# A fifth seven-product pair in the second column half of Down, and a new order of its pairs

## The chip, the cores and the metric

The kernel runs on one core of a Trainium2 chip. Its time is the device time in microseconds (us), the median of several runs. TensorE (PE in the profile) does the matmuls, PEld are its weight loads, VectorE is DVE, ScalarE is ACT, GpSimd is POOL, and SyncE (SP) issues the loads.

## The reference, cut to what matters

One block of a streaming encoder on x of 256 frames by 2048 features, in float32: a half-step SwiGLU FFN, a mixing part (gated DeltaNet and chunked attention, merged), and a second half-step FFN. The FFN is what matters here:

```python
def swiglu(h, w_gate, w_up, w_down):
    return (jax.nn.silu(h @ w_gate) * (h @ w_up)) @ w_down

h = rms_norm(x, ffn1_norm[l])
x = x + 0.5 * swiglu(h, ffn1_w_gate[l], ffn1_w_up[l], ffn1_w_down[l])
```

with a hidden width of 5504. The last matmul, by w_down, is called Down.

## The kernel before

**Products of float32 numbers.** Each weight and each activation is split into a high part and a low part in a rounded format, `hi` (a cast by ScalarE) and `lo = src - hi` (a subtraction by VectorE). A product (`product`, L456) is three matmuls, hi x hi (L462), hi x lo (L463), lo x hi (L464), each with a 128x128 activation block as the loaded operand and 512 columns of weights as the moving one.

**Pairs, plain and fast.** The contraction runs over k tiles of 128, two at a time: a pair. With the two blocks of 128 frames and two groups of 512 columns, a pair is a 2x2 by 2x2 product of blocks. A plain pair does it in eight block products (24 matmuls of 512 columns). A fast pair does it in seven (21 matmuls), by sums and differences of blocks in the manner of Strassen and Winograd. A fast pair needs sums of the activation blocks (`act_sums`, and for Down `bank_sums`, L573) and of the weight blocks.

**Preparing the weights of a pair.** `load` (L344) takes a buffer `raw` and has SP fetch the pair's weights, 1 MB in two DMAs. `begin` (L362) does the rest up to ScalarE's casts, and `prepare` (L426) the subtractions:
- plain: one cast `wh` (L380) and one subtraction `wl` (L434), each 128x2048; three buffers (raw, wh, wl);
- fast: three VectorE operations for the sums `s` (L406 to L408), casts of two pieces of raw (`w`, `v`, L411) and of `s` (`sh`, L413), and the subtractions `w`, `v` and `sl` (L434); five large buffers (raw, s, w1, sh, sl) and a small one of a ring of two (v).

**The order.** `plan` (L279) lists all pairs in order of use with a flag plain or fast, and a step takes the next one. Weights are loaded up to two pairs ahead of the one being prepared. Which buffer and which place in an engine's queue an operation gets is settled when the program is built. All large tiles come from one ring of 22 buffers, 8 KB per partition each (`heap`, L61): the weights, the activations x of the FFN (four fast pairs with a buffer each, four plain ones with half a buffer each), four hidden tiles of a chunk, and the block sums of hidden pairs (two pairs to a buffer).

**The FFN (L593).** Groups of 512 hidden columns run through gate/up (`gate_up`, eleven groups in all), in chunks of 4, 4 and 3 groups (`CHUNKS`). Behind each chunk comes its part of Down. The first two chunks have 16 k tiles, that is, pairs 0 to 7; their Down does the 2048 output columns in two halves, d = 0 and d = 2, of two groups of 512 columns each. Each half is one call of `seven` (L489): it takes the pairs in the order `js`, those in `fast` by seven products. Behind the last fast pair the banks that only fast pairs use are combined on ScalarE and VectorE (L531 to L535) while the remaining plain pair runs; the results leave by accumulating DMAs of GpSimd (L628). Behind the second half the next chunk's gate/up groups follow; the first two of a chunk have four fast pairs each (0, 2, 4, 6), the others three (0, 2, 4).

Before, both halves of a 16-k-tile chunk had the fast pairs 2, 3, 5, 6. The first half took the pairs in the order 0, 1, 2, 4, 3, 7, 5, 6 and the second in their natural order. The hidden tiles' transposes and block sums are jobs (`hidden`, L597) that run some steps behind gate/up, the last two of a chunk in the first steps of Down's first half.

In the profile Down's outputs are `pd`, gate/up's `pf`, hidden tiles `hid`, their block sums `hs`, the sums' scratch `shid`, the FFN's x `xf` (fast) and `xr` (plain).

Of the kernel before, what the change touches and what calls it, by code (L numbers as in the profile page):

```python
# [20 lines left out]
KD = D // P  # L21
# [9 lines left out]
FOUR = (0, 2, 4, 6)  # L31
DOWN = (2, 4, 6)
SECOND = (1, 3, 0, 2, 4, 5, 6, 7)
DEEP = (2, 3, 5, 6)
LAST = (1, 3)
APART = (0, 1, 2, 4, 3, 7, 5, 6)
FIRST = (1, 3, 5, 7, 0, 2, 4, 6)
QUAD = {2: (0, 0), 3: (1, 0), 4: (0, 1), 8: (1, 1)}
CHUNKS = ((0, 4), (4, 8), (8, 11))
# [5 lines left out]
def block_kernel(ctx: ExitStack, tc: tile.TileContext, a: dict, out: bass.AP):  # L45
# [220 lines left out]
    FG = [(c, min(4, KF - c)) for c in range(0, KF, 4)]  # L266
# [6 lines left out]
    def pairs_of(f, i):  # L273
        return range(KD // 2) if i else FIRST if f == "1" else SECOND

    def down_pairs(a0, a1):
        return DEEP if a1 < len(FG) else LAST

    def plan():  # L279

        for f in "12":
            for a0, a1 in CHUNKS:
                for i in range(a0, a1):
                    c, m = FG[i]
                    js = pairs_of(f, i)
                    gu = zip(*(t_pieces(a[w + f], c, m, 0, KD, [2 * j for j in js]) for w in ("wg", "wu")))
                    for j, p in zip(js, gu):
                        yield j in fast_pairs(f, i), p
                k0, k1 = FG[a0][0], sum(FG[a1 - 1])
                cols = lambda d, js=None: t_pieces(a["wd" + f], 4 * d, 4, k0, k1, js and [k0 + 2 * j for j in js])  # L290
                for d in (0, 2):
                    if a1 < len(FG):
                        js = range(KD // 2) if d else APART
                        yield from sevens(cols(d, js), cols(d + 1, js), DEEP, js)
                    elif d == 0:
                        yield from sevens(cols(0), cols(1), LAST, range(6))
                    else:
                        yield from twos(cols(2))
                        yield from twos(cols(3))
            if f == "2":  # L300
                return
            yield from mixing()
# [5 lines left out]
    def sevens(one, two, fast=DOWN, pairs=range(KD // 2)):  # L308
        for j, pieces in zip(pairs, zip(one, two)):
            yield j in fast, pieces  # L310
# [178 lines left out]
    def seven(nm, n, fast, act, jobs=(), feed=None, pairs=range(KD // 2), out=None, base=None, kt=KD):  # L489

        size = {b: len(fast) for b in range(1, 9)}
        for b in (2, 3, 4, 8):
            size[b] += kt - 2 * len(fast)
        size[8] -= len(fast)
        done = dict.fromkeys(size, 0)
        banks = {}

        def add(b, act, wt):  # L500
            if b not in banks:
                banks[b] = (acc_bank if b < 5 else core_bank)(f"p{nm}_{b}")[:, :n]
            done[b] += 1
            product(banks[b], act, wt, done[b] == 1, done[b] == size[b])

        ev = {}
        idle = 0
        for at_pair, j in enumerate(pairs):
            if j in fast:
                ps = take_weights()  # L510
                for at, (b, i7, w) in enumerate(ps):
                    add(b, act(j, i7), w)
                    if at == 3:
                        tick()
            else:
                for s in range(2):
                    wh, wl, _ = take_weights()
                    if feed and s == 0:
                        feed(at_pair)
                    for k, w in enumerate(zip(wh, wl)):  # L520
                        for t in range(2):
                            add((2, 4, 3, 8)[2 * s + t], act(j, 2 * k + t), w)
                    idle += 1
                    if idle > 3 and jobs and j > max(fast, default=-1):
                        jobs.popleft()()
                    while at_pair == KD // 2 - 1 and s == 1 and jobs:
                        jobs.popleft()()
            if fast and j == fast[-1]:
                idle = 1
                g0, u0, g1, u1 = (wide(f"e{nm}_{x}", n) for x in range(4))  # L530
                nc.scalar.copy(g0, banks[1])  # L531
                nc.vector.tensor_add(u0, banks[6], g0)
                nc.vector.tensor_add(g1, banks[7], u0)
                nc.vector.tensor_add(u1, banks[5], g1)
                nc.vector.tensor_add(u0, banks[5], u0)  # L535
                ev = {2: g0, 3: u0, 4: g1, 8: u1}
                if base:
                    for b, x in base.items():
                        nc.vector.tensor_add(ev[b], x, ev[b])
        if out:  # L540
            for b, put in out.items():
                put(ev[b])
                e = wide(f"e{nm}_{b}", n)
                nc.scalar.copy(e, banks[b])  # L544
                put(e)
            return None
        if not fast:
            return banks
        for b in (2, 3, 4, 8):
            nc.vector.tensor_add(ev[b], banks[b], ev[b])  # L550
        return ev
# [41 lines left out]
    def ffn(nm, xr, nxt, feed):  # L593
        f = "1" if nxt else "2"
        jobs = deque()

        def hidden(hb, us, m, c0, more):  # L597

            for c, mm, ps in turn(lambda t: us[t][:, c0 * P :], min(2, m - c0), f"{hb.name}_{c0}"):
                dst = hb[:, c0 : c0 + mm]  # L600
                split_to(dst[:, :, 0, :], dst[:, :, 1, :], ps)
                if more is not None:
                    bank_sums(ps, more, f"{hb.name}_{c0}")

        for a0, a1 in CHUNKS:
            hid, fast, sums, half = [], down_pairs(a0, a1), {}, None
            for i in range(a0, a1):
                m = FG[i][1]
                us = gate_up(nm, f, i, xr, jobs, feed if i == 0 else None)
                hb = heap([P, 4, 2, T], F32R, f"hid{nm}_{i}")  # L610
                hid.append(hb)
                for c0 in range(0, m, 2):
                    j = 2 * (i - a0) + c0 // 2
                    if j in fast:
                        half = heap([P, 2, 2, 4, P], F32R, f"hs{nm}_{i}{j}") if half is None else half
                        sums[j], half = (half[:, 0], half) if len(sums) % 2 == 0 else (half[:, 1], None)
                    jobs.append(lambda hb=hb, us=us, m=m, c0=c0, s=sums.get(j): hidden(hb, us, m, c0, s))
            n = 3
            while jobs:
                after(n, jobs.popleft())  # L620
                n += 1
            last = a1 == len(FG)
            act = quads(hid)
            block = lambda j, b: act(2 * j + b // 2, b % 2) if b < 4 else [sums[j][:, s, b - 4] for s in range(2)]
            kt = sum(FG[a1 - 1]) - FG[a0][0]
            for d in (0,) if last else (0, 2):
                out = {
                    b: lambda e, dst=xd[d + dd][t]: nc.gpsimd.dma_start(dst, e, accum_op=ALU.add)  # L628
                    for b, (dd, t) in QUAD.items()
                }  # L630
                js = range(6) if last else range(KD // 2) if d else APART
                seven(f"d{nm}_{a0}{d}", 512, fast, block, pairs=js, out=out, kt=kt)
            if not last:
                continue

            def again(d):
                xs = fetch(d, f"{nm}{a0}")
                if nxt:
                    nxt.square(d, xs)
                    after(3, lambda: nxt.turn(d, xs))  # L640
                else:
                    after(3, lambda: store(d, xs))

            for d in range(2):
                after(3 + d, lambda d=d: again(d))
            for d in range(2, 4):
                pd = pair(f"pd{nm}_{a0}{d}")
                xs = fetch(d, f"{nm}{a0}")
                gemm(pd, sum(FG[a1 - 1]) - FG[a0][0], act, 512)
                for t in range(2):  # L650
                    nc.vector.tensor_add(xs[t], xs[t], pd[t])
                if not last:
                    put(xs, d)
                elif nxt:
                    norm(nxt, d, xs)
                elif d < 3:
                    after(3, lambda d=d, xs=xs: store(d, xs))
                else:
                    store(d, xs)
# [620 lines left out]
    block = lambda j, b: mq(2 * j + b // 2, b % 2) if b < 4 else [ms[j][:, s, b - 4] for s in range(2)]  # L1280
# [91 lines left out]
```

## Time and profile before

| what | value |
| --- | --- |
| time, median of 3 runs | 2103.79 us (2103.19 to 2105.52) |
| the profiled execution: span from first to last instruction | 2101.9 us |
| granted TensorE clock | 1.000 |
| PE busy, matmuls | 2086.3 us (99%), 9711 |
| PEld busy | 1738.0 us (83%) |
| DVE busy | 1837.8 us (87%), 2074 instructions |
| ACT busy | 1205.7 us (57%) |
| POOL busy | 78.8 us (4%) |
| HBM | 407.72 MB read, 28.32 MB written |

No time is listed for the profiled execution beside its span; the span stands 1.9 us under the median of the runs. A row of the timeline gives the start, the duration, the engine, the line, the operation, the tiles as out<-in, the shapes, and a count; in brackets stands the idle time of the engine ahead of it and who ended it. In a table by stretches the columns are the length of the stretch and each engine's busy time with its count of instructions. A row of the view by groups gives busy time, mean duration in ns, and idle time ahead of it. Rows of waits give the total, the count and the longest.

### The profile page before, as it was taken

How to read it: one execution, taken by the hardware profiler on the slowest of the kernel's cores; microseconds unless marked ns; L12 is line 12 of the kernel's file. 1: busy time of each engine (PE TensorE's matmuls, PEld its weight loads, DVE VectorE, ACT ScalarE, POOL GpSimd, SP SyncE). 2: the span in 40 equal slices, each digit the busy share in tenths (PEclk: the TensorE clock that was granted, in tenths of full speed). 3: DMA queues.
4: the chain of work that ended last, by engine and by line, in shares of the span. 5: the costliest groups of instructions: out<-in, count | busy, mean ns of one | idle time of the engine just before them, and what ended most of it. 6: DMA issues, size and time to landing. Idle time of an engine off the chain costs nothing.

```text
span 2101.9 us, 25811 instructions
## 1 busy us (share of the span) xinstructions
PE 2086.3 (99%) x9711; PEld 1738.0 (83%) x9711; DVE 1837.8 (87%) x2074; ACT 1205.7 (57%) x1254; POOL 78.8 (4%) x93
## 2 busy tenths in 40 slices
PE   8999999999999999999999999999999999999999
PEld 6888788887898988888888888888887888888897
DVE  6998999989997788877885787999989999889994
ACT  6755565646555655657555555556555555556552
POOL 0000110002001000000010000000000200011001
PEclk9999999999999999999999999999999999999999
DMA  9655895649858755644554466767655975569576
GB/s 317 219 189 181 246 270 196 206 148 277 254 189 247 256 183 178 225 156 142 164 179 159 143 201 219 236 200 226 213 188 169 283 236 194 180 189 309 178 224 161
DMA packets 399932, 437.73 MB, mean 208 GB/s; under 512 B 14896, under 2 KB 372544, under 8 KB 399552
## 3 DMA queue, kind: packets, MB, share of 16 engines
q1 hardware_dynamic: 388288, 415.12, 61.2%
q0 software_dynamic: 11520, 20.98, 5.8%
q8 instruction: 76, 1.25, 0.3%
q14 instruction: 48, 0.39, 0.1%
HBM read 407.72 MB, written 28.32 MB: 207 GB/s over the span
## 4 chain that ended last, share of the span: by engine, by line
PE 93%; DVE 3%; DMA 2%; SPq 1%; ACT 1%; issue 1%; DVEq 0%; ACTq 0%
PE pf L462 14%; PE pf L464 14%; PE pf L463 14%; PE pd L463 6%; PE pd L462 6%; PE pd L464 6%; PE pg L463 2%; PE pg L464 2%; PE pg L462 2%; PE pc L462 2%; PE pc L464 2%; PE pc L463 2%; DMA raw<-wd 1%; PE pwo L462 1%; PE pwo L464 1%; PE pwo L463 1%
## 5 line engine op out<-in xcount | busy, mean ns | idle before, releaser
L434 DVE TENSOR_TENSOR wl<-raw,wh 128x2048 fp32r<-128x2048 f32 (+5 forms) x267 | 571.2, 2147 | 56.6 <-issue 11.7
L380 ACT CAST wh<-raw 128x2048 fp32r<-128x2048 f32 (+5 forms) x267 | 476.2, 1799 | 91.7 <-PE pg L463 15.0
L413 ACT CAST sh<-s 128x2048 fp32r<-128x2048 f32 (+1 forms) x130 | 246.6, 1897 | 336.5 <-DVE s L408 332.5
L434 DVE TENSOR_TENSOR sl<-s,sh 128x2048 fp32r<-128x2048 f32 (+1 forms) x130 | 293.1, 2260 | 23.1 <-PE pd L463 10.1
L463 PE MATMUL pf<-wl,xr 128*128 128x512 f32 (+1 forms) x704 | 271.0, 385 | 0.3 <-DVE wl L434 0.2
L464 PE MATMUL pf<-wh,xr 128*128 128x512 f32 (+1 forms) x704 | 270.6, 384 | 0.0
L462 PE MATMUL pf<-wh,xr 128*128 128x512 f32 (+1 forms) x704 | 261.6, 386 | 3.0 <-ACT xr L182 2.4
L411 ACT CAST w<-raw 128x1024 fp32r<-128x1024 f32 (+1 forms) x130 | 135.3, 1041 | 82.5 <-issue 20.6
L406 DVE TENSOR_TENSOR s<-raw 128x1024 f32<-128x1024 f32 (+1 forms) x130 | 156.8, 1206 | 17.6 <-PE pd L463 9.2
L434 DVE TENSOR_TENSOR w<-raw,w 128x1024 fp32r<-128x1024 f32 (+1 forms) x130 | 156.9, 1207 | 11.5 <-ACT w L411 11.2
L463 PE MATMUL pd<-wl,hid 128*128 128x512 f32 x400 | 157.2, 393 | 0.0
L462 PEld LDWEIGHTS pf<-wh,xr 128*128 128x128 f32 x704 | 132.0, 188 | 29.6 <-ACT xr L182 2.8
L464 PE MATMUL pd<-wh,hid 128*128 128x512 f32 x400 | 156.4, 391 | 0.0
L463 PEld LDWEIGHTS pf<-wl,xr 128*128 128x128 f32 x704 | 132.2, 188 | 25.8 <-DVE wl L434 1.0
L464 PEld LDWEIGHTS pf<-wh,xr 128*128 128x128 f32 x704 | 132.1, 188 | 25.2 <-DVE xr L183 0.2
L462 PE MATMUL pd<-wh,hid 128*128 128x512 f32 x400 | 146.8, 394 | 0.8 <-ACT ed L544 0.6
L628 POOL DMA_DIRECT2D xd<-ed x80 | 70.3, 1065 | 1574.4 <-ACT ed L531 1471.2
L411 ACT CAST v<-raw 128x512 fp32r<-128x512 f32 (+1 forms) x130 | 79.9, 614 | 57.8 <-PE pf L464 33.4
L463 PE MATMUL pf<-sl,xf 128*128 128x512 f32 (+1 forms) x292 | 112.3, 384 | 0.0
L464 PE MATMUL pf<-sh,xf 128*128 128x512 f32 (+1 forms) x292 | 112.0, 385 | 0.0
L462 PE MATMUL pf<-sh,xf 128*128 128x512 f32 (+1 forms) x292 | 110.3, 386 | 0.1
L463 PEld LDWEIGHTS pd<-wl,hid 128*128 128x128 f32 x400 | 75.1, 188 | 19.1 <-DVE wl L434 4.3
(542 smaller groups left out, 4335.7 us busy)
## 6 DMA issues: line engine op xcount, KB each, us to landing
raw<-wd SPq DMA_DIRECT2D x168, 512.0 KB, 5.0
raw<-wg SPq DMA_DIRECT2D x159, 512.0 KB, 4.5
raw<-wu SPq DMA_DIRECT2D x159, 512.0 KB, 5.7
raw<-wgt SPq DMA_DIRECT2D x64, 512.0 KB, 4.7
raw<-wa SPq DMA_DIRECT2D x48, 512.0 KB, 4.5
raw<-wc SPq DMA_DIRECT2D x48, 512.0 KB, 4.7
xd<-ed POOLq DMA_DIRECT2D x80, 256.0 KB, 6.9
raw<-wbr SPq DMA_DIRECT2D x32, 512.0 KB, 4.8
```

Of the source, the lines that this page charges most:

```text
L380: nc.scalar.copy(hi, src)
L406: nc.vector.tensor_sub(S[:, 0:2], R[:, 1], R[:, :, 0])
L411: nc.scalar.copy(hi, src)
L413: nc.scalar.copy(sh, s)
L434: nc.vector.tensor_sub(lo, src, f32(hi))
L462: nc.tensor.matmul(dst, ah, wh, start=start, stop=False)
L463: nc.tensor.matmul(dst, ah, wl, start=False, stop=False)
L464: nc.tensor.matmul(dst, al, wh, start=False, stop=stop)
L628: b: lambda e, dst=xd[d + dd][t]: nc.gpsimd.dma_start(dst, e, accum_op=ALU.add)
```

## The change

In the two chunks of 16 k tiles, in both FFNs, the second column half of Down has a fifth fast pair, pair 7, and takes the pairs in the order 0, 2, 3, 1, 5, 6, 7, 4. The first half keeps its pairs and its order. The hidden blocks of pair 7 get their sums (`down_pairs(a1, 2)` decides for which pairs a sum is made), which takes a third buffer for sums in these chunks.

```diff
-DEEP = (2, 3, 5, 6)
+DEEP = ((2, 3, 5, 6), (2, 3, 5, 6, 7))
 LAST = (1, 3)
-APART = (0, 1, 2, 4, 3, 7, 5, 6)
+APART = ((0, 1, 2, 4, 3, 7, 5, 6), (0, 2, 3, 1, 5, 6, 7, 4))
...
-    def down_pairs(a0, a1):
-        return DEEP if a1 < len(FG) else LAST
+    def down_pairs(a1, d):
+        return DEEP[d // 2] if a1 < len(FG) else LAST
...
                     if a1 < len(FG):
-                        js = range(KD // 2) if d else APART
-                        yield from sevens(cols(d, js), cols(d + 1, js), DEEP, js)
+                        js = APART[d // 2]
+                        yield from sevens(cols(d, js), cols(d + 1, js), DEEP[d // 2], js)
...
-            hid, fast, sums, half = [], down_pairs(a0, a1), {}, None
+            hid, fast, sums, half = [], down_pairs(a1, 2), {}, None
...
-                js = range(6) if last else range(KD // 2) if d else APART
-                seven(f"d{nm}_{a0}{d}", 512, fast, block, pairs=js, out=out, kt=kt)
+                js, some = range(6) if last else APART[d // 2], down_pairs(a1, d)
+                at_end = [j for j in js if j in some]
+                seven(f"d{nm}_{a0}{d}", 512, at_end, block, pairs=js, out=out, kt=kt)
```

## The prediction

> **What bounds the kernel now.** I read the page first: the shares of the engines, then the granted clock, then the chain that ended last.
>
> ```profile
> span 2101.9 us, 25811 instructions
> PE 2086.3 (99%) x9711; PEld 1738.0 (83%) x9711; DVE 1837.8 (87%) x2074; ACT 1205.7 (57%) x1254; POOL 78.8 (4%) x93
> PEclk9999999999999999999999999999999999999999
> PE 93%; DVE 3%; DMA 2%; SPq 1%; ACT 1%; issue 1%; DVEq 0%; ACTq 0%
> ```
>
> TensorE (PE) carries 93% of the chain at full clock. VectorE (DVE) at 87% is not far behind, and a mean over the span says nothing of one stage. So I then read the timeline for the price of a matmul.
>
> ```profile
> 260.50 0.39 PE L462 MATMUL pd<-w,hid 128*128 128x512 f32 x1
> ...
> 265.04 0.39 PE L464 MATMUL pd<-v,hs 128*128 128x512 f32 x1
> 265.26 0.39 PE L462 MATMUL pd<-wh,hid 128*128 128x512 f32 x1
> ```
>
> These are the first and last of the 21 matmuls of one fast pair and the first of the pair behind it: (265.26 - 260.50) / 21 = 0.227 us from start to start. The 0.39 us of a row overlaps its neighbours and is no price. A fast pair costs TensorE 4.76 us, a plain one 24 x 0.227 = 5.44 us.
>
> Next the busy times by stage: Down's first column half, its second half (where the change is), and the two gate/up groups behind it. A few matmuls of the next stage run early, so the third border is not sharp.
>
> ```profile
> core 0: us, PE busy (x) PEld busy (x) DVE busy (x) ACT busy (x) POOL busy (x), PEclk, DMA share, GB/s
> 186.08:228.67 42.59, 42.59 (x189) 34.33 (x188) 38.22 (x42) 22.76 (x22) 1.01 (x1) 1.00 0.57 176
> 228.67:266.17 37.50, 37.07 (x161) 29.80 (x160) 35.82 (x35) 21.95 (x21) 7.84 (x9) 1.00 1.05 281
> 266.17:311.96 45.79, 45.79 (x201) 37.38 (x200) 45.48 (x42) 28.79 (x26) 5.31 (x7) 1.00 0.94 272
> 311.96:353.56 41.60, 41.60 (x189) 34.52 (x188) 40.93 (x39) 23.32 (x21) 0.00 (x0) 1.00 0.62 203
> ```
>
> VectorE is idle for 37.50 - 35.82 = 1.68 us in the second half, 0.31 us in the next group and 0.67 us in the one after. From here to 353 us two engines are full together. What decides is the lead: how long before TensorE asks for a low part VectorE has finished it. VectorE's rows:
>
> ```profile
> 238.76 0.69 DVE L408 TENSOR_TENSOR s<-raw,s 128x512 f32<-128x512 f32 x1
> 241.06 4.49 DVE L434 TENSOR_TENSOR sl<-s,sh 128x2048 fp32r<-128x2048 f32 x2 [1.61 <-PE pd L463]
> ...
> 255.88 4.49 DVE L434 TENSOR_TENSOR sl<-s,sh 128x2048 fp32r<-128x2048 f32 x2
> ...
> 268.96 2.28 DVE L434 TENSOR_TENSOR sl<-s,sh 128x2048 fp32r<-128x2048 f32 x1
> ```
>
> and TensorE's first reads of three of these tiles (pair 5, pair 6, and pair 0 of the next group):
>
> ```profile
> 258.69 0.39 PE L463 MATMUL pd<-sl,hs 128*128 128x512 f32 x1
> 262.09 0.39 PE L463 MATMUL pd<-sl,hs 128*128 128x512 f32 x1
> 272.68 0.39 PE L463 MATMUL pf<-sl,xf 128*128 128x512 f32 x1
> ```
>
> The two subtractions from 255.88 end at about 258.1 and 260.37: leads of 0.5 and 1.7 us. The one from 268.96 ends at 271.24: 1.44 us. TensorE already waits in this stage, as its weight loads show:
>
> ```profile
> 243.41 0.19 PEld L463 LDWEIGHTS pd<-sl,hs 128*128 128x128 f32 x1 [0.32 <-DVE sl L434]
> ...
> 251.73 0.30 PEld L462 LDWEIGHTS pd<-sh,hs 128*128 128x128 f32 x2 [0.74 <-ACT sh L413]
> ```
>
> So the place of the change is one where VectorE has almost nothing to give. The other three places look the same; each has one idle gap of VectorE, for TensorE to release a buffer:
>
> ```profile
> 493.60 4.49 DVE L434 TENSOR_TENSOR sl<-s,sh 128x2048 fp32r<-128x2048 f32 x2 [1.75 <-PE pd L463]
> 1636.04 2.29 DVE L434 TENSOR_TENSOR sl<-s,sh 128x2048 fp32r<-128x2048 f32 x1 [1.88 <-PE pd L463]
> 1888.35 2.29 DVE L434 TENSOR_TENSOR sl<-s,sh 128x2048 fp32r<-128x2048 f32 x1 [1.57 <-PE pd L463]
> ```
>
> **The change part by part.** It acts at four places: two 16-k-tile chunks in each of two FFNs.
>
> *TensorE.* Pair 7 goes from 24 matmuls to 21: 3 x 0.227 = 0.68 us a place, 12 matmuls and 2.7 us in all, on the path as long as TensorE is fed.
>
> *VectorE, weights.* A run without idle time gives both prices:
>
> ```profile
> 320.08 1.22 DVE L406 TENSOR_TENSOR s<-raw 128x1024 f32<-128x1024 f32 x1
> ...
> 324.15 2.28 DVE L434 TENSOR_TENSOR wl<-raw,wh 128x2048 fp32r<-128x2048 f32 x1
> 326.36 2.28 DVE L434 TENSOR_TENSOR sl<-s,sh 128x2048 fp32r<-128x2048 f32 x1
> 328.56 1.22 DVE L406 TENSOR_TENSOR s<-raw 128x1024 f32<-128x1024 f32 x1
> ```
>
> From one s to the next, one fast and one plain pair are prepared: 8.48 us. The plain one is the wl row, 2.21 us to the next start; the fast one is the other 6.27 us. Turning pair 7 fast adds 4.06 us of VectorE, where 0.68 us of TensorE goes. Shift of the lead: 4.74 us a place.
>
> *How much shows.* VectorE runs without idle time from 241.06 through 311.96 but for 0.31 us. Its sl for pair 0 of the next group, done at 271.24, moves to 275.30; TensorE asks at 272.68 - 0.68 = 272.00. It waits 3.30 us. If the 1.61 us gap ahead of 241.06 could be filled, 1.69 us. The gap is a wait for a buffer, and the change leaves one buffer fewer (below), so I take 3.0, near the upper end. Once TensorE has waited, the pairs behind have their old leads, or larger ones: pair 2's sl ends at 279.72 and is read at 283.18, a lead of 3.46.
>
> ```profile
> 277.44 2.28 DVE L434 TENSOR_TENSOR sl<-s,sh 128x2048 fp32r<-128x2048 f32 x1
> ...
> 283.18 0.39 PE L463 MATMUL pf<-sl,xf 128*128 128x512 f32 x1
> ```
>
> *The order.* Before, the half began with two plain pairs; now one plain pair is followed by two fast ones, and 5, 6, 7 stand together. That is 2 x 6.27 + 2.21 = 14.75 us of VectorE against 14.96 of TensorE, then 18.81 against 14.28. The order moves the wait to an earlier pair or splits it; the sum up to the next group stays. The loads change order with it, same count and bytes on SP's queue. The partial results still leave after the seventh pair, with a plain pair behind it: nothing. POOL's accumulating DMAs stay.
>
> *The sums of pair 7's hidden blocks.* They are made early in the first half. Nearest rows, pair 6's:
>
> ```profile
> 194.72 0.29 DVE L147 TENSOR_TENSOR shid<-shid,hid 128x128 f32<-128x128 f32 x1 [0.34 <-ACT shid L577]
> ...
> 195.45 0.28 DVE L150 TENSOR_TENSOR shid<-hid,shid 128x128 f32<-128x128 f32 x1
> ...
> 196.60 0.68 DVE L131 TENSOR_TENSOR hs<-shid,hs 128x512 fp32r<-128x512 f32 x1
> ```
>
> At most 4 x 0.28 + 0.68 = 1.8 us a place. The 42.59 - 38.22 = 4.37 us that VectorE is idle in the first half hide it; uncovered, they cost 1.8.
>
> *ScalarE.* Casts of 1.05 + 0.62 + 1.92 replace one of 1.91, 1.7 us more; ScalarE is idle 15.55 us of the second half (37.50 - 21.95). Nothing.
>
> ```profile
> L380 ACT CAST wh<-raw 128x2048 fp32r<-128x2048 f32 x227 | 431.5, 1911 | 89.9 <-PE pg L463 15.0 <-DVE wl L434 9.7 <-PE pc L463 9.4
> L413 ACT CAST sh<-s 128x2048 fp32r<-128x2048 f32 x124 | 237.7, 1917 | 321.4 <-DVE s L408 317.4 <-DVE gs_pl L864 3.0 <-DVE rs_rn L107 1.1
> L411 ACT CAST w<-raw 128x1024 fp32r<-128x1024 f32 x124 | 130.3, 1051 | 82.5 <-issue 20.6 <-PE pd L464 11.9 <-PE pf L463 7.8
> L411 ACT CAST v<-raw 128x512 fp32r<-128x512 f32 x124 | 76.8, 619 | 47.2 <-PE pf L464 22.7 <-DMA raw<-wu 6.5 <-issue 5.3
> ```
>
> *Buffers.* Of the 22 large ones, Down holds 6 for x, 4 for hidden, 2 for sums; the fifth fast pair takes a third, so 9 instead of 10 stay for weights, from early in the first half to the end of the second. VectorE and SP both wait for releases there:
>
> ```profile
> DVE sl L434 <- PE pd L463: 2.5, 3, 1.6
> DVE s L406 <- PE pd L463: 2.3, 2, 1.7
> ...
> SPq L357 <- PE pd L464: 45.9, 10, 8.2
> ```
>
> No row shows 9 buffers. Lower bound nothing, since a later load or subtraction can fall into a wait that is there anyway; upper bound for the first half: its waits of VectorE, 2.5 + 2.3 - 1.61 = 3.2 us, grow as much again. I take 0.3, near the lower end, since VectorE idles 4.37 us in that half.
>
> *Sum.* A place: -0.68 + 3.0 + 0.3 = +2.6; four: +10.5 us. The profiled span of 2101.9 becomes 2112.4. The median of the three runs, 2103.79, stands 1.9 above that span: 2114.3 us. With the ends of the two unknown terms, 4 x (-0.68 + 1.69) = +4 and 4 x (-0.68 + 3.30 + 3.2) = +23: 2108 to 2127.
>
> **The rivals.**
>
> *Covered (not slower).* Mechanism: VectorE does the 4.06 us in time it now idles away, the 1.61 us gap and part of the first half's 4.37. It decides when at least 4.74 - 1.44 = 3.30 us are worked ahead before the second half's fifth pair. Then only the matmuls show: 2103.8 - 2.7 = 2101.1. For it: the idle time is there, right ahead. Against: each gap ends with TensorE releasing a buffer, so VectorE had nowhere to write. If the new order also removed the waits of 0.32 and 0.74 us, four times 1.06 more would go: 2096.9.
>
> *VectorE is the bound throughout.* Every added microsecond of VectorE shows and the matmuls' saving nothing: 4 x (4.06 + 1.8) = +23.4, 2127.2 us. For it: 45.48 busy of 45.79 in the group behind. Against: the idle 4.37 of the first half, where the 1.8 falls. The Trainium skill, page Perfetto Trace Analysis, section "Identifying the Most-Contended Engine", has a rule that speaks this way: judge TensorE by its weight loads, not by matmul busy time, and the others by occupancy, and the highest is the one to relieve. By that rule the 87% of DVE against 83% of PEld, in the first fence, makes VectorE the engine that this change should not load. The trace agrees within these stages; over the span DVE's 13% of idle time speaks against it.
>
> *Buffers bind.* If the flow of weights went with the count of buffers, the two halves, 42.59 + 37.50 = 80.1 us with 10, would take 10/9 of it with 9: +8.9 a place, +35.6, 2139.4 us. For it: SP's waits for releases. Against: with 10 buffers VectorE waits for releases in 2.5 + 2.3 = 4.8 us of the 80.1, so the flow is not bound by them throughout.
>
> **How the numbers follow.** Less than 0.2%, 4.2 us, can't be told from no change here. Forecast, 2108 to 2127: 0.53. Covered, within 4.2 us of before: 0.25; covered with waits removed, below 2099.6: 0.07. VectorE throughout: 0.09. Buffers: 0.06. Faster 0.07, same 0.25, slower 0.68. The predicted time is the forecast's, 2114.3. The range from 2101 (covered) to 2126 leaves out the faster case, half of the one at 2127 and the buffers, under 2 in 10.
>
> **What would show it.** Right: 9699 matmuls, VectorE's busy time up by up to 4 x (4.06 + 1.8) = 23.4 us; waits of PE or PEld for DVE (sl, wl, s) of about 3 us near the end of each second half and the start of the next group; that half and the next group together longer by 2 to 3 us. Wrong: no new waits there and VectorE's gap near 241 filled (covered); waits of DVE and SP for PE releases up by microseconds in the first half (buffers). What would make the number wrong most easily is how far VectorE can use its gap, worth 1.6 us a place, 6.4 in all.

## The result, and the profile after

The kernel became slower: 2163.53 us (median of 4 runs, 2162.98 to 2164.31) beside 2104.31 us for the kernel before in the same session, a ratio of 1.0279 with a 95% interval of 1.0267 to 1.0292. That is +59.2 us where +10.5 was forecast; the sign was right, the size was not, and the time lies outside the range of 2101 to 2126. The profiled execution took 2164.03 us.

The page of the kernel after, its span, busy times and shares of the chain:

```profile
span 2162.3 us, 25863 instructions
PE 2108.3 (98%) x9699; PEld 1747.6 (81%) x9699; DVE 1861.5 (86%) x2114; ACT 1216.5 (56%) x1270; POOL 78.6 (4%) x93
PE 89%; DVE 4%; issue 2%; ACT 2%; DMA 2%; SPq 1%; DVEq 0%; ACTq 0%
```

The work is as forecast: 12 matmuls fewer, and VectorE busy 1861.5 - 1837.8 = 23.7 us longer (23.4 was the bound). But the span grew by 60.4 us, so VectorE's *idle* time grew by 36.7 us. And 12 matmuls fewer gave 22 us *more* busy time of TensorE, most of which the clock will explain.

The busy times by stage of the kernel after, with the same columns as before: first half, second half, next group, the group behind it, and then two short stretches inside the halves.

```profile
186.09:233.81 47.72, 44.86 (x190) 35.16 (x188) 37.47 (x47) 22.76 (x25) 1.01 (x1) 0.96 0.45 142
233.81:279.02 45.21, 40.10 (x158) 31.54 (x157) 41.18 (x40) 23.74 (x24) 7.87 (x9) 0.92 0.90 238
279.02:326.21 47.19, 45.77 (x202) 37.39 (x200) 46.87 (x42) 29.74 (x25) 5.24 (x6) 1.00 0.94 275
326.21:367.80 41.59, 41.59 (x189) 34.53 (x188) 40.91 (x39) 23.30 (x21) 0.00 (x0) 1.00 0.62 203
217.64:221.05 3.41, 3.09 (x7) 2.48 (x8) 3.09 (x4) 0.27 (x1) 0.00 (x0) 0.50 0.88 293
258.60:262.01 3.41, 3.41 (x10) 2.63 (x9) 3.38 (x4) 0.53 (x1) 0.00 (x0) 0.50 0.61 196
```

The first half took 47.72 us instead of 42.59, although it has the same pairs in the same order. The second took 45.21 instead of 37.50, the next group 47.19 instead of 45.79, and the group after that is as it was (41.59 beside 41.60). At this first of the four places that is 5.1 + 7.7 + 1.4 = 14.2 us. VectorE is idle for 47.72 - 37.47 = 10.25 us of the first half (4.37 before) and for 45.21 - 41.18 = 4.03 us of the second (1.68 before), where the prediction had it nearly full. An engine that gets more work and has more idle time is waiting for something else. The waits of both halves name it (engine and line, who ended the wait, then total us, count, longest):

```profile
...
ACT w L411 <- PE pd L463: 12.6, 3, 6.6
ACT v L411 <- PE pd L464: 11.5, 4, 4.9
ACT sh L413 <- DVE s L408: 10.4, 5, 2.9
PEld pd L462 <- ACT sh L413: 8.6, 4, 3.0
PE pd L462 <- ACT sh L413: 7.0, 3, 2.7
...
DVE sl L434 <- PE pd L464: 4.6, 1, 4.6
DVE sl L434 <- PE pd L463: 4.3, 3, 3.9
...
ACT w L411 <- PE pd L464: 1.7, 2, 1.2
```

The same casts' waits for TensorE in both halves of the kernel before, where none of `v` is listed:

```profile
ACT w L411 <- PE pd L464: 3.4, 2, 1.8
...
ACT w L411 <- PE pd L463: 1.2, 1, 1.2
```

So `w` and `v` waited 25.8 us for TensorE in place of 4.6. Read from the top, this is a circle. ScalarE's casts `w` and `v` need a free buffer to write into (`v` one of the small ring), and wait up to 6.6 us until a TensorE matmul (L463, L464), the last reader of one, has released it. TensorE waits for ScalarE's next cast, `sh`. The timeline of the kernel after shows it in the first half and, from 255.46 on, in the second:

```profile
217.96 1.22 PE L462 MATMUL pd<-sh,hs 128*128 128x512 f32 x2 [1.85 <-ACT sh L413]
...
220.14 0.69 DVE L408 TENSOR_TENSOR s<-raw,s 128x512 f32<-128x512 f32 x1
224.49 1.05 ACT L411 CAST w<-raw 128x1024 fp32r<-128x1024 f32 x1 [6.59 <-PE pd L463]
225.47 2.29 DVE L434 TENSOR_TENSOR sl<-s,sh 128x2048 fp32r<-128x2048 f32 x1 [4.64 <-PE pd L464]
...
255.46 0.39 PE L464 MATMUL pd<-w,hid 128*128 128x512 f32 x1
258.23 0.92 PE L462 MATMUL pd<-sh,hs 128*128 128x512 f32 x2 [2.38 <-ACT sh L413]
258.95 0.63 PE L463 MATMUL pd<-wl,hid 128*128 128x512 f32 x1
...
261.51 0.63 PE L464 MATMUL pd<-wh,hid 128*128 128x512 f32 x1
```

VectorE finishes `s` at 220.83 and starts nothing until 225.47; ScalarE sits idle for 6.59 us ahead of its cast. TensorE itself stops for 1.85 us in the first half and for 2.38 us in the second, and behind the second stop its matmuls start (261.51 - 258.95) / 6 = 0.427 us apart instead of 0.227. The last two rows of the table by stage say why: for 3.41 us the granted clock was 0.50. The page's row of clocks, all nines as before, cannot show so short a stretch.

Counted over the trace's clock records, up to the last matmul, the kernel before has none of these; the kernel after has 11 stretches, 41.0 us together. At full clock that work takes 0.227 / 0.427 of the time, so the half clock cost up to 41.0 x (1 - 0.227 / 0.427) = 19 us (less where TensorE would have waited anyway). It is no cause of its own: it stands behind stops of TensorE.

### The profile page after: what moved, and what is told of

It reads as the page before. It is cut to its first block, busy times and chain, and to the rows that moved or that the text cites. A ratio compares the mean times of both kernels' runs of the same rounds, so it can differ in the third digit from the quotient of the medians.

```text
span 2162.3 us, 25863 instructions
## 1 busy us (share of the span) xinstructions
PE 2108.3 (98%) x9699; PEld 1747.6 (81%) x9699; DVE 1861.5 (86%) x2114; ACT 1216.5 (56%) x1270; POOL 78.6 (4%) x93
## 3 DMA queue, kind: packets, MB, share of 16 engines
q1 hardware_dynamic: 388288, 415.12, 59.2%
## 4 chain that ended last, share of the span: by engine, by line
PE 89%; DVE 4%; issue 2%; ACT 2%; DMA 2%; SPq 1%; DVEq 0%; ACTq 0%
PE pf L462 13%; PE pf L463 13%; PE pf L464 13%; PE pd L463 6%; PE pd L464 6%; PE pd L462 6%; PE pg L463 2%; PE pg L464 2%; PE pg L462 2%; PE pc L462 2%; PE pc L464 2%; PE pc L463 2%; ACT sh L413 1%; PE pwo L462 1%; DMA raw<-wd 1%
## 5 line engine op out<-in xcount | busy, mean ns | idle before, releaser
L434 DVE TENSOR_TENSOR wl<-raw,wh 128x2048 fp32r<-128x2048 f32 (+5 forms) x263 | 561.7, 2143 | 55.8 <-issue 11.7
L380 ACT CAST wh<-raw 128x2048 fp32r<-128x2048 f32 (+5 forms) x263 | 468.5, 1797 | 91.5 <-PE pg L463 15.0
L413 ACT CAST sh<-s 128x2048 fp32r<-128x2048 f32 (+1 forms) x134 | 253.8, 1894 | 303.7 <-DVE s L408 299.5
L434 DVE TENSOR_TENSOR sl<-s,sh 128x2048 fp32r<-128x2048 f32 (+1 forms) x134 | 302.4, 2260 | 49.7 <-PE pd L464 20.2
L463 PE MATMUL pf<-wl,xr 128*128 128x512 f32 (+1 forms) x704 | 271.0, 385 | 0.2 <-DVE wl L434 0.2
L464 PE MATMUL pf<-wh,xr 128*128 128x512 f32 (+1 forms) x704 | 270.6, 384 | 0.0
L434 DVE TENSOR_TENSOR w<-raw,w 128x1024 fp32r<-128x1024 f32 (+1 forms) x134 | 161.7, 1206 | 18.1 <-ACT w L411 17.9
L406 DVE TENSOR_TENSOR s<-raw 128x1024 f32<-128x1024 f32 (+1 forms) x134 | 161.5, 1205 | 10.5 <-PE pg L463 4.3
L463 PEld LDWEIGHTS pf<-wl,xr 128*128 128x128 f32 x704 | 132.1, 188 | 25.5 <-DVE wl L434 0.7
L464 PEld LDWEIGHTS pf<-wh,xr 128*128 128x128 f32 x704 | 132.2, 188 | 25.3 <-DVE xr L183 0.2
L463 PE MATMUL pd<-wl,hid 128*128 128x512 f32 x368 | 150.7, 409 | 0.0
L464 PE MATMUL pd<-wh,hid 128*128 128x512 f32 x368 | 150.3, 409 | 0.0
L462 PE MATMUL pd<-wh,hid 128*128 128x512 f32 x368 | 141.1, 406 | 0.1
L463 PE MATMUL pf<-sl,xf 128*128 128x512 f32 (+1 forms) x292 | 112.4, 385 | 0.0
L464 PE MATMUL pf<-sh,xf 128*128 128x512 f32 (+1 forms) x292 | 112.0, 385 | 0.0
L434 DVE TENSOR_TENSOR v<-raw,v 128x512 fp32r<-128x512 f32 (+1 forms) x134 | 90.7, 677 | 11.7 <-ACT v L411 11.6
```

Source lines behind the costliest of these rows:

```text
L380: nc.scalar.copy(hi, src)
L406: nc.vector.tensor_sub(S[:, 0:2], R[:, 1], R[:, :, 0])
L413: nc.scalar.copy(sh, s)
L434: nc.vector.tensor_sub(lo, src, f32(hi))
L462: nc.tensor.matmul(dst, ah, wh, start=start, stop=False)
L463: nc.tensor.matmul(dst, ah, wl, start=False, stop=False)
```

## The experiments

The theories were: the buffer alone (9 large ones instead of 10 for weights), the fifth pair's VectorE work, the new order, the order of TensorE's queue, and an interaction of fifth pair and buffer. Each kernel's ratio is to the kernel before, run on the same chip beside it. "The change" is the kernel after.

**Making pair 7's sums, without using them.** The kernel before, plus the third sums tile, filled and read once.

```diff
+            fast = (*fast, 7) if a1 < len(FG) else fast
+                nc.scalar.copy(held, f32(sums[7][:, 0, 0, 0:1]))
```

> The kernel before (four fast pairs, natural order) with the third sums buffer of the change: pair 7's sums are made in the first half, kept to the end of the second by one small read there, and used by no product. Theory BUFFER (one buffer fewer for weights makes the wait): the first half is longer by about 5 us at each place as it is after the change (47.7 against 42.6), the second half by some us more, 2130 to 2150 us in all. Rival ENGINES (the fifth pair's work on VectorE and ScalarE makes the wait): only the sums' 1.8 us a place, mostly hidden, 2104 to 2111.

Measured: 2108.55 us beside 2103.80, ratio 1.0021 (1.0011 to 1.0032). That lies where the rival expected it, but as a test of the buffer the run failed. The read that was to keep the buffer ran early, at 199.0 us and so in the first half, and gave it back:

```profile
L637 ACT COPY held<-hs x4: 191/191/192, 199.0 to 1849.1; 128x1 f32<-128x1 f32 x4
```

What is left is a price of making the sums: 4.75 us, 1.2 us a place. That includes a buffer held for a short while.

**The change with its buffer given back.** Pair 7's sums go into a third buffer of the small ring, so that 10 large ones stay (the roomy kernel below); room for it came from small tiles of the mixing part.

```diff
-NH = 2
+NH = 3
+                        if len(sums) == 4:
+                            sums[j] = half_tile([P, 2, 4, P], F32R, f"hs{nm}_{i}{j}")
```

> The changed kernel, with pair 7's sums in a third buffer of the small ring (4 KB) in place of a large one. The room comes from the constants: the four masks of the mixing part are loaded when they are used, into the same ring. So 10 large buffers stay for weights, and the fifth pair and the new order are as changed. Theory BUFFER: the first half back at 42.6 us, the second near what the prediction's ledger gave (a wait of 1.7 to 3.3 less 0.68), 2101 to 2114 us. ENGINES or ORDER: within 10 us of 2163.

Measured: 2130.71 us, ratio 1.0126 (1.0107 to 1.0146), between the two expectations. More than half of the loss, 59.2 - 26.9 = 32.3 us, is gone with one buffer; 26.9 us stay with fifth pair and order.

**TensorE's queue in order.** In the built program the first five matmuls of a fast pair stand between matmuls of the plain pair ahead of it. Here each pair's products are bound behind the last product of the pair before.

```diff
+                    with queued(behind):
+                        add(b, act(j, i7), w)
```

> The changed kernel with 9 buffers, but TensorE's queue is bound to take Down's pairs one after the other: in the 16-k-tile Downs no product of a plain pair stands behind the first products of the next fast one. Theory QUEUE (TensorE stops at early products of the next fast pair while 20 matmuls of a plain pair stand ready behind them): most of the 14.8 us a place goes, 2110 to 2130 us. If the buffers alone decide when a fast pair is ready, the wait only moves behind the plain pair: 2155 to 2165.

Measured: 2160.98 us, ratio 1.0268 (1.0248 to 1.0289), beside 1.0279 for the change. The queue theory falls. The windows below, both halves and the next group of this kernel, are cut with other borders (178 and 181 matmuls in the last two, where the table above has 158 and 202), so only their sum compares: 138.56 us beside 140.12.

```profile
185.93:232.43 46.50, 42.81 (x189) 34.19 (x188) 38.27 (x48) 22.49 (x23) 1.00 (x1) 1.00 0.48 149
232.43:283.69 51.26, 44.92 (x178) 35.13 (x177) 47.17 (x44) 28.85 (x27) 10.47 (x12) 0.93 0.89 243
283.69:324.49 40.80, 40.80 (x181) 33.78 (x180) 40.23 (x37) 24.80 (x22) 2.64 (x3) 1.00 0.93 272
```

**The order alone.** Four fast pairs as before, in the new order.

```diff
-DEEP = ((2, 3, 5, 6), (2, 3, 5, 6, 7))
+DEEP = ((2, 3, 5, 6), (2, 3, 5, 6))
```

> The new order 0, 2, 3, 1, 5, 6, 7, 4 with the four fast pairs of before (7 plain, no third sums buffer). Theory BUFFER: no wait of note, 2102 to 2110 us. Rival ORDER (two fast pairs after one plain pair come too early): 2115 to 2140.

Measured: 2115.60 us (2 runs, 2113.58 and 2117.63), ratio 1.0053 (1.0032 to 1.0073). So the order alone costs 11.8 us (6.7 to 15.4 by the interval), with no work added. Its windows for the same three stages:

```profile
187.33:229.83 42.50, 42.50 (x189) 34.34 (x188) 38.11 (x45) 21.88 (x22) 1.00 (x1) 1.00 0.56 174
229.83:273.86 44.03, 41.88 (x181) 33.55 (x180) 42.62 (x38) 27.13 (x26) 10.45 (x12) 1.00 1.02 273
273.86:314.74 40.88, 40.88 (x182) 33.71 (x180) 40.88 (x38) 26.99 (x24) 2.65 (x3) 1.00 0.90 271
```

Together 127.41 us, 1.53 more than the 125.88 of before; TensorE is idle 2.15 us of the second half. Four such places would be 6.1 us. But the places differ: in the profiled execution, 9.9 us longer than the one before, they are 1.5, 2.1, 4.2 and 1.4 us longer, each taken over the same count of matmuls. The third holds a stop of TensorE of 2.54 us and behind it 3.41 us at half clock, which cost at most 1.6 us.

**The buffer alone, this time kept.** As the first experiment, but the third sums tile is read at the end of the second half, behind a result that VectorE has only then.

```diff
-                nc.scalar.copy(held, f32(sums[7][:, 0, 0, 0:1]))
+                nc.vector.tensor_add(held, e[:, 0:1], f32(sums[7][:, 0, 0, 0:1]))
```

> As held, but the read of pair 7's sums also takes the last result of the second half, so that the third sums buffer is really kept to its end: four fast pairs, natural order, 9 buffers for weights in Down. In held the small read ran early, at 199 us, and gave the buffer back; that kernel showed the making of the sums alone. Theory BUFFER ALONE: the whole difference between the change and roomy, 33 us, on top of held's 2108.6: 2135 to 2145 us, and the first half at about 47 us. Rival BUFFER WITH FIFTH PAIR (9 buffers are short only when five fast pairs pass through them): 2108 to 2120.

Measured: 2157.47 us beside 2103.85, ratio 1.0250 (1.0229 to 1.0270), more than either theory expected. The tile's row, the windows of the three stages, and the waits of both halves of this kernel:

```profile
L637 DVE TENSOR_TENSOR held<-ed,hs x4: 147/150/150, 289.5 to 1978.4; 128x1 f32<-128x1 f32 x4
```

```profile
185.88:233.79 47.91, 44.98 (x190) 35.26 (x188) 36.78 (x44) 22.93 (x23) 1.00 (x1) 0.96 0.45 143
233.79:280.79 47.00, 40.42 (x161) 31.15 (x160) 39.55 (x38) 23.29 (x22) 7.82 (x9) 0.93 0.88 238
280.79:326.23 45.44, 45.44 (x201) 37.46 (x200) 45.10 (x43) 28.26 (x25) 5.26 (x6) 1.00 0.94 273
```

```profile
...
ACT w L411 <- PE pd L463: 12.1, 2, 6.7
DVE sl L434 <- PE pd L464: 8.3, 3, 4.8
ACT v L411 <- PE pd L464: 8.1, 2, 4.9
```

This is the picture of the kernel after, without a fifth fast pair and without a new order: the first half at 47.91 us, the same casts waiting 6.7 and 4.9 us for the same matmuls, clock 0.96 and 0.93. The two kernels differ in how long one buffer is held (and in which engine makes a read of under 0.2 us): (2157.47 - 2103.85) - (2108.55 - 2103.80) = 48.9 us. The buffer alone does it, at 12.2 us a place. Two things may make that a little high: the read runs at 289.5 us, in the next group, where the kernel after reads its third sums for the last time by 277.9 us; and ScalarE waits 4.7 us in all for the four reads. The longer first half lies ahead of both. No interaction with the fifth pair is needed.

**Ten buffers, fifth pair, and the two plain pairs ahead.** The roomy kernel in the order 0, 1, 2, 3, 5, 6, 7, 4.

```diff
-APART = ((0, 1, 2, 4, 3, 7, 5, 6), (0, 2, 3, 1, 5, 6, 7, 4))
+APART = ((0, 1, 2, 4, 3, 7, 5, 6), (0, 1, 2, 3, 5, 6, 7, 4))
```

> roomy (fifth fast pair, 10 large buffers) with pair 1 back ahead of the fast pairs: 0, 1, 2, 3, 5, 6, 7, 4. Theory ORDER HURTS (order4 took 11.8 us more than before with no other change of work): 2113 to 2123. Rival VECTORE (its work until the next group is the same whatever the order, so the wait only moves): 2126 to 2135.

Measured: 2137.94 us, ratio 1.0157 (1.0137 to 1.0177), beside 1.0126 with the new order. That is 34.1 us over the kernel before in place of 26.9. With five fast pairs the new order is by the medians the better of the two, though the intervals just overlap; with four it was worse than the old one. So the 11.8 us of the order alone may not be subtracted from the 26.9.

**The change in a ring of 23, and the kernel before in a ring of 23.** Six scratch tiles instead of eight and the room in the mixing part pay for a 23rd large buffer; with the third sums tile 10 stay for weights in the change, and 11 in the kernel before.

```diff
-NB = 22
+NB = 23
-        return tp.tile([P, 512], F32, name=name, tag="w", bufs=8)[:, :n]
+        return tp.tile([P, 512], F32, name=name, tag="w", bufs=6)[:, :n]
```

> The changed kernel with 23 large buffers in place of 22, so 10 for weights in Down, paid for by the constants' room and by 6 in place of 8 of the small scratch tiles through which results leave. Theory BUFFER: as roomy, 2122 to 2135, first half 42.5 to 44 us. If the 33 us of roomy came from something else in its layout (masks, third small buffer): near 2163.

> The kernel before with that layout: 23 large buffers (11 for weights in Down), 6 scratch tiles. Theory BUFFER: Down's waits of the kernel before (about 2 us a place beside the matmuls) shrink, 2094 to 2103 us. Rival: 10 buffers are enough for four fast pairs, 2102 to 2106; scratch tiles too few, 2107 to 2120.

Measured: the change 2127.42 us, ratio 1.0107 (1.0087 to 1.0127); the kernel before 2098.73 us beside 2103.85, ratio 0.9975 (0.9965 to 0.9985; 9 runs beside 12). The latter is faster than both kernels of this case. Windows of the change in the ring of 23, first place and then the second half and next group of the second place:

```profile
186.37:229.17 42.80, 42.45 (x190) 34.29 (x188) 37.66 (x45) 21.41 (x23) 1.00 (x1) 1.00 0.53 169
229.17:271.17 42.00, 37.76 (x159) 28.79 (x157) 38.84 (x37) 23.59 (x24) 7.78 (x9) 1.00 0.90 246
271.17:318.67 47.50, 46.01 (x202) 37.30 (x200) 47.25 (x43) 29.78 (x25) 5.28 (x7) 1.00 0.94 271
...
488.07:530.25 42.18, 37.96 (x159) 28.79 (x157) 38.82 (x37) 23.59 (x24) 7.78 (x9) 1.00 0.91 244
530.25:577.76 47.51, 46.02 (x201) 37.30 (x200) 47.23 (x43) 29.77 (x25) 5.28 (x7) 1.00 0.95 271
```

With 10 buffers the first half is back at 42.80 us, and in this kernel no clock is halved up to the last matmul. What stays is in the stage of the change: 42.00 + 47.50 = 89.50 us beside 37.50 + 45.79 = 83.29, +6.2 a place, four times 24.8 beside a measured 23.6. TensorE is idle for 4.24 us of this half, VectorE for 3.16; in the group behind it VectorE is full (47.25 of 47.50).

**Ten buffers, with VectorE's last additions left out.** The ring of 23; the four additions at the end of both halves are not made, and one bank is copied in their place.

```diff
+                if out and len(pairs) == KD // 2:
+                    g0 = wide(f"e{nm}_0", n)
+                    nc.scalar.copy(g0, banks[1])
+                    ev = dict.fromkeys((2, 3, 4, 8), g0)
+                    continue
```

> room_23 (fifth pair, new order, 10 large buffers in Down, 2127.4 us), with the four VectorE additions left out by which the banks of the fast pairs are combined at the end of both halves of a 16-k-tile Down (about 2.4 us of VectorE a half); the one ScalarE copy of bank 1 stays, its result leaves four times. Theory VECTORE (what is left of the loss with 10 buffers is VectorE's lack of time, as the prediction's ledger has it): each place gains 2.4 to 4.8 us, 2108 to 2118. Rival (buffers or order): 2124 to 2130.

Measured: 2122.59 us beside 2105.85, ratio 1.0082 (1.0051 to 1.0113), above the expectation. Its first place holds 6.8 us at half clock, against none in the kernel above. An undisturbed place, the second, can be compared row by row:

```profile
489.13:528.45 39.32, 36.67 (x159) 29.26 (x157) 36.62 (x34) 23.44 (x23) 7.52 (x9) 1.00 0.94 259
528.45:575.10 46.65, 45.67 (x202) 37.46 (x201) 45.40 (x39) 30.33 (x26) 3.48 (x4) 1.00 0.98 278
```

85.97 us instead of 42.18 + 47.51 = 89.69: 3.7 us less. VectorE's busy time fell by 38.82 + 47.23 - 36.62 - 45.40 = 4.0 us. So nearly all VectorE work taken out here came off the time. Over the same counts of matmuls the third place gains 3.8 us and the fourth 2.3; the first, with its half clock, loses 1.4. With 10 buffers it is VectorE, then, that bounds most of this stage, with two reservations: by the medians the whole kernel gains only 4.8 us, with intervals that overlap, and the edit also takes one scratch tile where four were taken, a part that no run separates.

**Loads one pair ahead instead of two.** The change with 9 buffers, of which fewer hold weights not yet worked on.

```diff
-    PREP, LOAD = 5, 2
+    PREP, LOAD = 5, 1
```

> The changed kernel (9 buffers in Down) with weights loaded one pair ahead instead of two, in the whole kernel, so that one buffer fewer waits for or holds data not yet needed. If the buffers that loads hold ahead are what starves the preparation: the first half back under 44 us and Down's waits mostly gone, though other stages may lose. If the transfer of about 5 us then lies open: both halves as long as now or longer, 2160 to 2250 us.

Measured: 2168.47 us, ratio 1.0300 (1.0257 to 1.0342): no better. Both halves of this kernel:

```profile
185.95:228.75 42.80, 42.46 (x189) 34.29 (x188) 36.86 (x44) 22.60 (x24) 1.01 (x1) 1.00 0.53 169
228.75:275.35 46.60, 39.37 (x159) 30.19 (x157) 39.88 (x39) 23.31 (x22) 7.83 (x9) 0.93 0.84 221
```

The first half is back at its old length with 9 buffers, but the second is worse than the change's 45.21 us. The edit acts in the whole kernel, so its total says little of Down: taken over the same counts of matmuls, the four places together are 10.8 us shorter than in the change, and the rest of the kernel is some 18 us longer. It matters what the buffers hold, not only how many there are.

## Why the prediction was wrong in size

**Buffers: the step that failed.** The prediction put the ring's loss at 0.3 us a place, between 0 and 3.2. The runs show 12.2 us a place where the buffer is taken away alone, and, with the fifth pair there, 59.2 - 23.6 = 35.6 us, or 8.9 a place (32.3 us, 8.1 a place, against the roomy kernel). The upper bound rested on letting the waits that were there grow as much again. But the wait of 1.6 us with 10 buffers said little of 9: the longest waits for a release were then 4.6 to 6.7 us. That they last until TensorE is done with a buffer of a pair further on is argued, not shown. The idle 4.37 us of VectorE in the first half, named as cover, was hardly any: for 3.1 us of it VectorE waited for TensorE to release a buffer, and with 9 buffers for 8.9 us of 10.25. A count from the code fits: two fast pairs in a row need five large buffers each, ten in all, which 10 hold and 9 do not. It would explain why the step from 10 to 9 costs 49 us and the one from 10 to 11 brings 5; no run isolates it.

**Buffers bind, the rival.** Its mechanism, given 6 in 100, is the one that came true. Its sign was seen for VectorE, whose waits for TensorE's releases in the first half rose from 3.1 to 8.9 us, but not for SP, whose such waits went from 31.1 to 28.1 us; those of ScalarE's casts `w` and `v`, which it did not name, rose from 2.8 to 12.1. That its +8.9 a place is also the price measured beside the fifth pair is luck: it scaled the two halves by 10/9, and the buffer alone cost 12.2. It was still 24 us short, since it priced the fifth pair at nothing. In that sense no case of the prediction was whole: each took one term and left out the others.

**The wait behind VectorE: mis-sized.** Predicted 3.0 us a place, so +2.3 with the matmuls' saving. With 10 buffers the kernel lost 23.6 us, 5.9 a place, of which the sums explain at most 1.2; the wait is 5.4 to 6.6 us. The mechanism stands, as leaving out VectorE's additions showed in three of the four places. The shift of the lead, 4.74 us, was taken to be softened by leads and a gap ahead of it; the runs show no softening. It came in good part by another way than forecast: with the ring of 23 the weight loads of TensorE waited 5.3 us for `sh` (1.1 before) and 4.4 us for VectorE's low parts (0.6 before) in the first place's second half and next group. The order is in it too, in a share that stays open.

**The order: wrong.** "The sum up to the next group stays" did not hold: the order alone cost 11.8 us. The reasoning counted VectorE's and TensorE's time per pair. What it missed stays open: the count of buffers above does not explain it, since the natural order has two fast pairs in a row as well (2, 3 and 5, 6) and the kernel before and the one with the new order alone both have 10 buffers.

**The sums: not covered.** Nothing was taken for them, with 1.8 us a place as the price if uncovered; 1.2 a place was measured, a short hold of the buffer included.

**TensorE's 12 matmuls and VectorE's +23.4 us** were right; the matmuls' 2.7 us were lost in waits. **ScalarE at nothing** was right as to work, yet the waits of TensorE's weight loads name ScalarE (`sh` L413, 8.6 us). The rows above that one in the view of waits show ScalarE waiting itself, for TensorE's releases and for VectorE's `s`.

**VectorE the bound throughout** gave 2127.2; the change with 10 buffers measured 2127.42 and 2130.71. With the buffer back, that rival was the closest, in part by luck: what the order costs is in the measured times and not in its sum. The rule it cited (the Trainium skill, page Perfetto Trace Analysis, section "Identifying the Most-Contended Engine") names VectorE, and in the ring of 23 the trace agrees, with VectorE busy 47.25 of 47.50 us in the next group; with 9 buffers it does not, where VectorE's idle time in the two halves rose from 6.05 to 14.28 us. The same page, section "Optimization Strategy", says that a gap that keeps coming back on the engine that should be full can mean too little memory for the next tile; the kernel that only held a buffer agrees, with +48.9 us.

**The clock** was no step at all. The prediction took 0.227 us for every matmul; 41.0 us of the span ran at 0.427, which cost up to 19 us.

Adding up, over the kernel before: fifth pair, its sums and the order with 10 buffers, +23.6 to +26.9; the tenth buffer, +35.6 to +32.3, which includes the up to 19 us of half clock. Open is how the first part divides between order and VectorE, and how much of the 9-buffer loss comes from the places and order of instructions, which are settled when the program is built, and how much from waits alone.

## What to carry to other kernels

When a change takes a buffer from a ring in which engines already wait for releases, do not scale the waits that are there: count how many buffers the next two pieces of work need at once, and if the new count is below it, do not expect the waits to stay small; here the longest grew from 1.8 us to between 4.6 and 6.7, about what TensorE takes for one pair. The count itself is argued here, not shown. Idle time of an engine is cover only if the engine has somewhere to write; look up who ended it. To price a buffer, hold one without using it, and see in the trace that it was really held; and try one more buffer before one more trick, which here gave the only gain (0.9975).

## What was not expected of the hardware

Stops of TensorE of 1.85 to 2.73 us stood beside the 11 stretches with a clock of 0.50, most of them 3.41 us long, at a matmul pitch of 0.427 us instead of 0.227. The kernel before had no such stretch, the kernel after 41.0 us of them, the kernel that only held the buffer 41.0, the change with loads one ahead 47.8, and the change in a ring of 23 none. But not every such stop was followed by one: the kernel after stops for 2.87 us up to 505.82 and stays at full clock, and a stop of 2.4 us near 21 us, which every kernel has, was followed by a half clock in the first experiment's kernel and not in the kernel before. Windows of 3.41 us of the kernel after, two that end where the clock fell and the two that hold the stop of 2.87 us:

```profile
214.23:217.64 3.41, 1.20 (x5) 0.34 (x3) 3.41 (x3) 1.63 (x1) 0.00 (x0) 1.00 0.16 28
255.19:258.60 3.41, 1.03 (x5) 0.52 (x5) 3.41 (x4) 2.32 (x2) 0.00 (x0) 1.00 1.09 368
500.95:504.36 3.41, 2.00 (x9) 1.23 (x7) 3.41 (x7) 1.94 (x4) 0.86 (x1) 1.00 1.11 313
504.36:507.77 3.41, 1.95 (x7) 1.34 (x8) 3.41 (x4) 2.87 (x4) 1.00 (x2) 1.00 0.77 105
```

Starts of the stretches lie whole multiples of 3.41 us apart (238.12 is 6 x 3.413 behind 217.64), and in the 3.41 us ahead of each of the 11 TensorE was busy for 20 to 48%. The stop of 2.87 us fell across two such windows, busy 59% and 57%. One window busy 46% (a stop of 2.21 us up to 528.61) was not followed by a half clock, so no sharp threshold can be given. The Trainium skill, page "TensorE: Matmul & The Clock Gate", section "What's actually happening", tells of a free-running window of 3413 ns and half the clock after a whole idle window; the length of 3.41 us agrees. That a whole idle window is needed does not: here 2.38 us between two matmuls, at 255.46 and 258.23, were enough, and the measurement decides. So a stop of 2 us can cost 1.6 us more behind it (3.41 x 0.468), by where it falls. In the profile's page it shows only as a longer "busy" time of TensorE: 2108.3 us for 9699 matmuls, beside 2089.2 us for as many in the ring of 23.
